# Two residual blocks in one kernel: the entry of the last FFN with its additions on two engines and its first round of gate and up in two merged steps

## The chip, the cores and the metric

The kernel runs on one core of one Trainium2 chip. The metric is device microseconds of one execution, and the time of a kernel is the median of several executions. The time before the change is 1148.94 us, the median of three executions (1146.13, 1148.94 and 1149.74). The profile is of a separate execution.

## The reference, cut to what matters

The reference chains two transformer blocks over 256 tokens of width 1024, all in float32. The first has two layers (an HGRN2 mixer, a band attention, and an FFN in each) and a final norm. The second has four attention mixers side by side, an output projection, and a convolutional FFN, which is the last thing computed. The change lies between that projection and the first products of this FFN:

```python
def _conv_ffn(x, w_gate, w_up, conv_w, conv_b, w_down):
    a = x @ w_gate                                   # 1024 x 4096
    a = lax.conv_general_dilated(a, conv_w[:, None, :], (1,), [(2, 0)], ...) + conv_b
    return (jax.nn.gelu(a, approximate=True) * (x @ w_up)) @ w_down

x = x + _rms_norm(mix @ w_out[l], attn_post_norm[l])
h = _rms_norm(x, ffn_pre_norm[l])
x = x + _rms_norm(_conv_ffn(h, ffn_w_gate[l], ffn_w_up[l], ffn_conv_w[l], ffn_conv_b[l], ffn_w_down[l]),
                  ffn_post_norm[l])
```

## The kernel before

**Split operands.** Every float32 product is made of three: an operand is split into a high part in a reduced format (hi) and the rest (lo), and PE computes hi·hi, hi·lo and lo·hi into the same PSUM bank (`mm3`, L257 to L260). Activations stand transposed, 128 features by 256 tokens in each of eight pieces k.

**Weight units and their pipeline.** Weights come as units of 128x1024 numbers. SP starts the DMA of a unit into one of seven raw buffers; ScalarE casts it to `w_hi` (L193) and VectorE subtracts to get `w_lo` (L195), each into one of four buffers. The program is a list of steps, each with the units it needs. `pump` runs before each step and emits the casts of units to come: it goes on while the number of units cast is at most `AHEAD` = 2 above the number of units used by the steps already emitted. So three units lie ready at any step, and the casts stand in the queues of ScalarE and VectorE at the place where the step before ended. Nothing reorders them after that: each engine works its queue in the order of the program.

**The FFN.** `ffn` makes 16 rounds. In round r, `lin_A` gives gate two steps and up two steps of one unit each (24 matmuls, k = 0 to 3 and then 4 to 7). When gate is complete, `conv_gate` runs: in round 0 it first calls `f2_scale`, which sums the squares of the residual on PE (`stat_mm`, L463) and takes 1/rms on ScalarE (L468, L469); then VectorE scales the gate (L1771), ScalarE and VectorE make the convolution (L1776 to L1779). `conv_gelu` (L1784 on ScalarE, L1786 on GpSimd) is emitted ahead of the first step of up. When up is complete, `mul_hidden` multiplies (L1073) and splits the hidden values (L1063, L1064). The down products of round r-1 follow those of round r.

**The entry.** `f2_start` (L1734) ends the projection: 1/rms of the mixer's output, then for each k the normed piece `nt` on VectorE (L1747, its source in PSUM), its addition to the residual on GpSimd (L1749), the high part on ScalarE (L1750) and, two pieces later, the low part on VectorE (L1752). Four squares of the residual on ScalarE follow (L1756), for `f2_scale`.

Of the kernel before, what the change touches and what calls it, by code (L numbers as in the profile page):

```python
# [10 lines left out]
F32 = mybir.dt.float32  # L11
F32R = mybir.dt.float32r
I32 = mybir.dt.int32
AF = mybir.ActivationFunctionType
OP = mybir.AluOpType
AX = mybir.AxisListType

P = 128
D = 1024
KT = 8  # L20
# [111 lines left out]
def kernel(ctx: ExitStack, tc: tile.TileContext, x, c, mod_w, mod_b, norm_mix, norm_ffn,  # L132
# [9 lines left out]
    PE, DV, SC, GP, SY = nc.tensor, nc.vector, nc.scalar, nc.gpsimd, nc.sync  # L142
# [12 lines left out]
    def bank(tag="b", bufs=3):  # L155
        return ps.tile([P, 512], F32, name="pb_" + tag, tag=tag, bufs=bufs)

    def acc_bank():
        return bank("acc", 4)
# [10 lines left out]
    def small(w, name, bufs=2, dt=F32):  # L170
        return wk.tile([P, w], dt, name=name, tag=name, bufs=bufs)
# [73 lines left out]
    def unit_A(w, r0, c0, k=4, width=256):  # L245
        ap = w[r0:r0 + k * P, c0:c0 + width].rearrange("(k p) m -> p k m", p=P)
        return Unit(k, width, [(0, width, ap)])
# [14 lines left out]
    def lin_A(w, c0, act, evac, alloc=bank):  # L262
        box = {}

        def half(i, u):
            if i == 0:
                box["p"] = alloc()
            p = box["p"]
            xhi, xlo = act()
            for k in range(4):  # L270
                for m in range(2):
                    mm3(p[:, 256 * m:256 * m + 256], u.hi[:, k, P * m:P * m + P], u.lo[:, k, P * m:P * m + P],
                        xhi[:, 4 * i + k], xlo[:, 4 * i + k], i == 0 and k == 0 and m == 0, i == 1 and k == 3)
            if i == 1:
                evac(p)

        return [Step(lambda u: half(0, u), [unit_A(w, 0, c0)], 2.6),
                Step(lambda u: half(1, u), [unit_A(w, 512, c0)], 2.6)]

    def lin_B(w, c0, act, evac):  # L280
        box = {}
# [88 lines left out]
    for n, ap in vb_list:  # L370
        r = rows(ap)
# [4 lines left out]
    def vcol(n):  # L376
        o, r, _ = VB[n]
        return vb_t[:, o:o + r]
# [7 lines left out]
    def hT():  # L386
        return hbox["h"]
# [201 lines left out]
    def act(tag):  # L589
        return lambda: ubox[tag]  # L590
# [437 lines left out]
    def ffn(w_gate, c_gate, w_up, c_up, w_out, rounds, u, gated, hidden, down, down_last, mid=None):  # L1028
        HB = {}
        gu = []  # L1030
        for r in range(rounds):
            def ev_gate(p, r=r):
                HB[r] = gated(r, p)

            def ev_up(p, r=r):
                HB[r] = hidden(r, HB[r], p)
            gate, up = lin_A(w_gate, c_gate + 256 * r, u, ev_gate), lin_A(w_up, c_up + 256 * r, u, ev_up)
            if mid:
                up[0].before = lambda r=r: mid(HB[r])
            gu.append(gate + up)  # L1040
        box = {}

        def dn(r, i, un):
            if r == 0 and i == 0:
                box["a"] = [acc_bank() for _ in range(4)]
            hi, lo = HB[r]
            down(box["a"], un, hi[:, i], lo[:, i], r == 0 and i == 0)

        def dn_last(ua, ub):
            down_last(box["a"], (ua, ub), HB[rounds - 1])  # L1050

        st = list(gu[0])
        for r in range(1, rounds):
            st += gu[r]
            for i in range(2):
                st.append(Step(lambda un, r=r, i=i: dn(r - 1, i, un), [unit_row(w_out, 256 * (r - 1) + P * i)], 2.6))
        st.append(Step(dn_last, [unit_row(w_out, 256 * (rounds - 1) + P * i) for i in range(2)], 5.2))
        return st

    def split_hidden(r, hid):  # L1060
        h = slot(5 + 2 * (r % 2), F32R)
# [215 lines left out]
    for i, g in ((2, g12[NF:]), (3, gemv_mod(1, 3, gemv_w)), (4, gemv_mod(1, 4, gemv_w))):  # L1277
        m = sum(len(s.units) for s in g)
# [12 lines left out]
    B_ = {}  # L1291
# [442 lines left out]
    def f2_start():  # L1734

        st = bank()
        stat_mm(st, stF[3], 0)
        PE.matmul(st[:, 0:256], lhsT=mean_d, rhs=stF[0][:, 0:256], start=False, stop=True)
        r = rstd_of(st[:, 0:256])
        hi = slot(1, F32R).rearrange("p (k t) -> p k t", k=KT)  # L1740
        lo = slot(2, F32R).rearrange("p (k t) -> p k t", k=KT)
        ubox["f2"] = (hi, lo)
        pre = vcol("ffn_pre")
        for k in range(KT + 2):
            if k < KT:
                t = small(256, "nt", 3)
                DV.scalar_tensor_tensor(t, B_["y", k // 2][:, 256 * (k % 2):256 * (k % 2) + 256],  # L1747
                                        vcol("attn_post")[:, k:k + 1], r, op0=OP.mult, op1=OP.mult)
                GP.tensor_add(hT()[:, k], hT()[:, k], t)  # L1749
                SC.activation(hi[:, k], hT()[:, k], AF.Identity, scale=pre[:, k:k + 1])  # L1750
            if k > 1:
                DV.scalar_tensor_tensor(lo[:, k - 2], hT()[:, k - 2], pre[:, k - 2:k - 1],  # L1752
                                        hi[:, k - 2].bitcast(F32), op0=OP.mult, op1=OP.subtract)
        for j in range(4):
            stF[j] = ph(768, "att", 4)[:, 0:512]
            SC.activation(stF[j], hT()[:, 2 * j:2 * j + 2].rearrange("p k t -> p (k t)"), AF.Square)  # L1756
# [135 lines left out]
```

## Time and profile before

| | |
|---|---|
| median of three executions | 1148.94 us (1146.13 to 1149.74) |
| the profiled execution | 1142.66 us, of which the span from the first to the last instruction is 1140.9 us |
| granted TensorE clock, mean over the span | 0.994 |
| busy in the span: PE, VectorE, ScalarE, GpSimd | 1098.1, 763.4, 573.4, 138.1 us |
| waits of PE for the entry's operand (L1750) | 2.9 us |

The profile names engines PE (TensorE; PEld is its weight load), DVE (VectorE), ACT (ScalarE), POOL (GpSimd) and SP (SyncE, which starts the weight DMAs). In its timeline a row has the start in us from the span's first instruction, the duration, engine, line, operation, the tiles out<-in, the shape, the count of merged instructions, and in brackets how long the engine sat idle before and what ended that. Matmuls overlap each other, so their pitch is shorter than their duration. A float32 matmul of `stat_mm` is two instructions in the profile.

### The profile page before, as it was taken

The numbers are of one execution on the slowest core, as the hardware profiler recorded it, in microseconds if no ns is written. First come the engines' busy times: TensorE is split into PE (matmuls) and PEld (weight loads), VectorE is DVE, ScalarE is ACT, GpSimd is POOL, SyncE is SP. The second block draws the span as 40 slices with busy tenths as digits, with TensorE's granted clock in tenths as the row PEclk, the third lists the DMA queues.
The fourth block names the chain that finished last, engine by engine and source line by source line (L and its number), as shares of the span: only waits on it lengthen the run. The fifth ranks groups of instructions, "written<-read, shape, count | busy, mean of one in ns | idle before, by whom it ended". The sixth has DMA issues, their size and how long they took to land.

```text
span 1140.9 us, 23598 instructions
## 1 busy us (share of the span) xinstructions
PE 1098.1 (96%) x9689; PEld 1014.4 (89%) x9689; DVE 763.4 (67%) x1237; ACT 573.4 (50%) x913; POOL 138.1 (12%) x201
## 2 busy tenths in 40 slices
PE   6988999999999999999999999999999999999997
PEld 4885789899999979888999999988888999999997
DVE  3586765787787688885564454667766766666666
ACT  3455464644444566555444444646555544554454
POOL 4044400000000001250000000013312100000000
PEclk9998999999999999999999999999999999999999
DMA  9976777798988777865766556773343656555651
GB/s 276 318 262 205 224 223 239 257 298 305 302 280 298 232 237 234 292 239 170 237 197 209 185 188 169 153 214 112 116 145 94 217 183 191 186 183 185 192 178 56
DMA packets 176125, 241.92 MB, mean 212 GB/s; under 512 B 18713, under 2 KB 142161, under 8 KB 176017
## 3 DMA queue, kind: packets, MB, share of 16 engines
q1 hardware_dynamic: 174928, 239.54, 66.4%
q8 instruction: 76, 1.25, 0.4%
q0 software_dynamic: 912, 0.81, 0.3%
q14 instruction: 33, 0.26, 0.1%
q10 hardware_dynamic: 176, 0.07, 0.0%
HBM read 239.33 MB, written 1.05 MB: 211 GB/s over the span
## 4 chain that ended last, share of the span: by engine, by line
PE 82%; DVE 6%; DMA 4%; ACT 4%; issue 2%; POOL 1%; SPq 0%; DVEq 0%; ACTq 0%; POOLq 0%
PE pb_b L258 14%; PE pb_b L260 14%; PE pb_b L259 14%; PE pb_acc L258 11%; PE pb_acc L260 10%; PE pb_acc L259 10%; DVE w_lo L195 2%; DMA w_raw<-in_a_w_in_dram 2%; ACT w_hi L193 2%; PE pb_b L463 1%; PE pb_b L1216 1%; DMA w_raw<-in_mod_w_dram 1%; DMA w_raw<-in_kv_w_dram 1%; PE pb_gv L524 1%; DVE nt L573 1%
## 5 line engine op out<-in xcount | busy, mean ns | idle before, releaser
L195 DVE TENSOR_TENSOR w_lo<-w_raw,w_hi 128x1024 fp32r<-128x1024 f32 (+1 forms) x335 | 409.3, 1246 | 172.7 <-ACT w_hi L193 172.0
L258 PE MATMUL pb_b<-s,w_hi 128*128 128x256 f32 x1488 | 419.4, 282 | 5.1 <-ACT s L1750 2.9
L260 PE MATMUL pb_b<-s,w_lo 128*128 128x256 f32 x1488 | 416.2, 280 | 1.6 <-DVE w_lo L195 1.5
L259 PE MATMUL pb_b<-s,w_hi 128*128 128x256 f32 x1488 | 417.3, 280 | 0.3
L193 ACT CAST w_hi<-w_raw 128x1024 fp32r<-128x1024 f32 (+1 forms) x336 | 342.1, 1043 | 79.3 <-DMA w_raw<-in_a_w_in_dram 19.2
L258 PEld LDWEIGHTS pb_b<-s,w_hi 128*128 128x128 f32 x1488 | 280.3, 188 | 12.7 <-issue 4.0
L260 PEld LDWEIGHTS pb_b<-s,w_lo 128*128 128x128 f32 x1488 | 280.3, 188 | 2.6 <-DVE w_lo L195 2.6
L259 PEld LDWEIGHTS pb_b<-s,w_hi 128*128 128x128 f32 x1488 | 280.3, 188 | 1.9 <-DVE s L585 0.7
L260 PE MATMUL pb_acc<-s,w_lo 128*128 128x256 f32 x656 | 183.4, 280 | 4.0 <-DVE w_lo L195 4.0
L258 PE MATMUL pb_acc<-s,w_hi 128*128 128x256 f32 x656 | 186.7, 285 | 0.6 <-ACT w_hi L193 0.6
L259 PE MATMUL pb_acc<-s,w_hi 128*128 128x256 f32 x656 | 183.1, 279 | 0.0
L258 PEld LDWEIGHTS pb_acc<-s,w_hi 128*128 128x128 f32 x656 | 123.3, 188 | 5.8 <-issue 3.5
L260 PEld LDWEIGHTS pb_acc<-s,w_lo 128*128 128x128 f32 x656 | 123.3, 188 | 4.8 <-DVE w_lo L195 4.8
L259 PEld LDWEIGHTS pb_acc<-s,w_hi 128*128 128x128 f32 x656 | 123.4, 188 | 0.2
L1209 POOL TENSOR_SCALAR att<-att,sm 128x128 f32<-128x128 f32 (+1 forms) x72 | 46.7, 668 | 619.4 <-DVE sm L1202 337.7
L1063 ACT CAST s<-sig 128x512 fp32r<-128x512 f32 x38 | 23.6, 621 | 115.9 <-DVE sig L1073 115.9
L258 PE MATMUL pb_acc<-w_hi,s 128*128 128x512 f32 x192 | 78.3, 408 | 1.7 <-ACT s L579 1.0
L259 PE MATMUL pb_acc<-w_lo,s 128*128 128x512 f32 x192 | 76.6, 399 | 0.8 <-DVE w_lo L195 0.8
L260 PE MATMUL pb_acc<-w_hi,s 128*128 128x512 f32 x192 | 76.5, 399 | 0.0
L1776 ACT ACTIVATE sig<-att,vb_t,vc_t 128x256 f32<-128x256 f32 x32 | 17.5, 595 | 75.4 <-DVE att L1771 75.4
L1069 ACT ACTIVATE sig<-pb_b 128x512 f32<-128x512 f32 x22 | 13.2, 598 | 77.8 <-PE pb_b L260 77.7
L1786 POOL TENSOR_TENSOR sig<-sig,rstd 128x512 f32<-128x512 f32 x16 | 22.7, 1420 | 237.2 <-ACT sig L1784 237.2
(373 smaller groups left out, 1255.7 us busy)
## 6 DMA issues: line engine op xcount, KB each, us to landing
w_raw<-in_mod_w_dram SPq DMA_DIRECT2D x96, 512.0 KB, 4.9
w_raw<-in_ffn_w_in_dram SPq DMA_DIRECT2D x88, 512.0 KB, 5.2
w_raw<-in_ffn_w_out_dram SPq DMA_DIRECT2D x44, 512.0 KB, 4.8
w_raw<-in_a_w_in_dram SPq DMA_DIRECT2D x32, 512.0 KB, 5.5
w_raw<-in_ffn_w_gate_dram SPq DMA_DIRECT2D x32, 512.0 KB, 3.8
w_raw<-in_ffn_w_up_dram SPq DMA_DIRECT2D x32, 512.0 KB, 5.3
w_raw<-in_ffn_w_down_dram SPq DMA_DIRECT2D x32, 512.0 KB, 3.6
w_raw<-in_kv_mod_w_dram SPq DMA_DIRECT2D x16, 512.0 KB, 5.8
```

Source lines behind the costliest of these rows:

```text
L193: SC.copy(hi, raw)
L195: DV.tensor_sub(lo, raw, hi.bitcast(F32))
L258: PE.matmul(o, lhsT=whi, rhs=xhi, start=start, stop=False, skip_group_check=True)
L259: PE.matmul(o, lhsT=whi, rhs=xlo, start=False, stop=False, skip_group_check=True)
L260: PE.matmul(o, lhsT=wlo, rhs=xhi, start=False, stop=stop, skip_group_check=True)
L463: PE.matmul(st[:, 0:256], lhsT=mean_d, rhs=sq[:, 256 * m:256 * m + 256], start=j == 0 and m == 0, stop=j == n - 1 and m == 1)
L524: PE.matmul(g[32 * j:32 * j + 32, 0:256], lhsT=by, rhs=r, start=start, stop=stop, tile_position=(0, 32 * j))
L1063: SC.copy(hi, hid)
L1069: SC.activation(sg, g, AF.Silu)
L1209: GP.tensor_scalar(t[:, i, cs], t[:, i, cs], r[:, 2 * b + i:2 * b + i + 1], 1.0, op0=OP.mult, op1=OP.mult)
L1776: SC.activation(zm, am, AF.Identity, bias=vcol("conv_b")[:, f:f + 1], scale=vc_t[:, 64 + f:65 + f])
L1786: GP.tensor_mul(zp, zp, rs_pair())
```

## The change

In `f2_start` the additions to the residual alternate: even pieces on VectorE, odd ones on GpSimd. The low parts are no longer made two pieces behind: those of pieces 0 to 3 come together after the fifth addition, those of 4 to 7 at the end. In the FFN with a `mid` function (the last one), the four steps of round 0 become two. Step i takes the units of gate and of up for four k at once, first all products with the high part of the operand (for gate and up, with both parts of the weights), then those with its low part. What followed each complete product (`conv_gate` with `f2_scale`, `conv_gelu`, `mul_hidden`) now comes in that order at the end of the second step.

```diff
@@ lin_A
-        return [Step(lambda u: half(0, u), [unit_A(w, 0, c0)], 2.6),
-                Step(lambda u: half(1, u), [unit_A(w, 512, c0)], 2.6)]
+        st = [Step(lambda u: half(0, u), [unit_A(w, 0, c0)], 2.6),
+              Step(lambda u: half(1, u), [unit_A(w, 512, c0)], 2.6)]
+        for s_ in st:
+            s_.evac = evac
+        return st
@@ ffn
         st = list(gu[0])
+        if mid:
+            st = [first_round(w_gate, c_gate, w_up, c_up, u, i, gu[0]) for i in range(2)]
...
+    def first_round(w_gate, c_gate, w_up, c_up, act, i, gu):
+
+        def f(ug, uu):
+            xhi, xlo = act()
+            for part in range(2):
+                for k in range(4):
+                    for u, n in ((ug, 0), (uu, 1)):
+                        if i == 0 and part == 0 and k == 0:
+                            first_bank[n] = bank()
+                        for m in range(2):
+                            o = first_bank[n][:, 256 * m:256 * m + 256]
+                            whi, wlo = (w[:, k, P * m:P * m + P] for w in (u.hi, u.lo))
+                            x_ = xhi[:, 4 * i + k]
+                            if part == 0:
+                                PE.matmul(o, lhsT=whi, rhs=x_, start=i == 0 and k == 0 and m == 0, stop=False,
+                                          skip_group_check=True)
+                                PE.matmul(o, lhsT=wlo, rhs=x_, start=False, stop=False, skip_group_check=True)
+                            else:
+                                PE.matmul(o, lhsT=whi, rhs=xlo[:, 4 * i + k], start=False, stop=i == 1 and k == 3,
+                                          skip_group_check=True)
+            if i == 1:
+                gu[0].evac(first_bank[0])
+                gu[2].before()
+                gu[2].evac(first_bank[1])
+        return Step(f, gu[i].units + gu[2 + i].units, 5.2)
@@ f2_start
-        for k in range(KT + 2):
-            if k < KT:
-                t = small(256, "nt", 3)
...
-                GP.tensor_add(hT()[:, k], hT()[:, k], t)
-                SC.activation(hi[:, k], hT()[:, k], AF.Identity, scale=pre[:, k:k + 1])
-            if k > 1:
...
+        for k in range(KT):
+            t = small(256, "nt", 3)
...
+            (GP if k % 2 else DV).tensor_add(hT()[:, k], hT()[:, k], t)
+            SC.activation(hi[:, k], hT()[:, k], AF.Identity, scale=pre[:, k:k + 1])
+            if k == 4:
+                for n in range(4):
+                    low(n)
+        for n in range(4, KT):
+            low(n)
```

In the order of VectorE at the entry (`nt` is the normed piece, `s0` the residual, `s1` and `s2` the high and the low part of the operand), there stood before:

```order
L1747 SCALAR_TENSOR_TENSOR nt_10461<-pb_acc_10118,vb_t_78,rstd_10456 128x256
L1747 SCALAR_TENSOR_TENSOR nt_10465<-pb_acc_10118,vb_t_78,rstd_10456 128x256
L1747 SCALAR_TENSOR_TENSOR nt_10469<-pb_acc_10119,vb_t_78,rstd_10456 128x256
L1752 SCALAR_TENSOR_TENSOR s2_10460<-s0_171,vb_t_78,s1_10459 128x256
L1747 SCALAR_TENSOR_TENSOR nt_10474<-pb_acc_10119,vb_t_78,rstd_10456 128x256
```

and there stand now:

```order
L1784 SCALAR_TENSOR_TENSOR nt_10461<-pb_acc_10118,vb_t_78,rstd_10456 128x256
L1786 TENSOR_TENSOR s0_171<-s0_171,nt_10461 128x256
L1784 SCALAR_TENSOR_TENSOR nt_10465<-pb_acc_10118,vb_t_78,rstd_10456 128x256
L1784 SCALAR_TENSOR_TENSOR nt_10469<-pb_acc_10119,vb_t_78,rstd_10456 128x256
L1786 TENSOR_TENSOR s0_171<-s0_171,nt_10469 128x256
L1784 SCALAR_TENSOR_TENSOR nt_10473<-pb_acc_10119,vb_t_78,rstd_10456 128x256
L1784 SCALAR_TENSOR_TENSOR nt_10477<-pb_acc_10120,vb_t_78,rstd_10456 128x256
L1786 TENSOR_TENSOR s0_171<-s0_171,nt_10477 128x256
L1779 SCALAR_TENSOR_TENSOR s2_10460<-s0_171,vb_t_78,s1_10459 128x256 x4
L1784 SCALAR_TENSOR_TENSOR nt_10485<-pb_acc_10120,vb_t_78,rstd_10456 128x256
```

Four additions came to VectorE, and four low parts now stand together ahead of the sixth normed piece.

In the order of ScalarE behind the entry's squares, `w_hi` of raw buffer 10202 is the second unit of up of round 0, that of 10251 and 10291 the first and second unit of gate of round 1, that of 10340 the first of up of round 1; `sig` is the gate on its way through convolution and gelu, `s5` the split hidden. Before:

```order
L1756 ACTIVATE att_10507<-s0_171 128x512
L193 CAST w_hi_10534<-w_raw_10202 128x1024
L468 ACTIVATE rstd_10573<-pb_b_10564,epsc_87 128x256
L469 ACTIVATE rstd_10573<-rstd_10573 128x256
L1776 ACTIVATE sig_10578<-att_10576,vb_t_78,vc_t_79 128x256 x2
L193 CAST w_hi_10585<-w_raw_10251 128x1024
L1784 ACT_TABLE_LOAD
L1784 ACTIVATE sig_10578<-sig_10578 128x512
L193 CAST w_hi_10618<-w_raw_10291 128x1024
L1063 CAST s5_10649<-sig_10578 128x512
L193 CAST w_hi_10652<-w_raw_10340 128x1024
```

and now:

```order
L1795 ACTIVATE att_10507<-s0_171 128x512
L193 CAST w_hi_10559<-w_raw_10202 128x1024
L193 CAST w_hi_10565<-w_raw_10251 128x1024
L471 ACTIVATE rstd_10628<-pb_b_10619,epsc_87 128x256
L472 ACTIVATE rstd_10628<-rstd_10628 128x256
L1815 ACTIVATE sig_10633<-att_10631,vb_t_78,vc_t_79 128x256 x2
L1823 ACT_TABLE_LOAD
L1823 ACTIVATE sig_10633<-sig_10633 128x512
L1096 CAST s5_10643<-sig_10633 128x512
L193 CAST w_hi_10646<-w_raw_10291 128x1024
L193 CAST w_hi_10652<-w_raw_10340 128x1024
```

The cast of the first unit of gate of round 1 moved ahead of the 1/rms, and that of the second unit (10291) moved behind the gelu and behind the cast of the hidden values.

In the order of PE at the start of the second merged step, whose first unit of weights is gate (10446) and whose second is up (10559), with their banks 10509 and 10514, there stand now:

```order
L1081 MATMUL pb_b_10509<-s1_10459,w_hi_10446 128x256
L1083 MATMUL pb_b_10509<-s1_10459,w_lo_10447 128x256
L1081 MATMUL pb_b_10509<-s1_10459,w_hi_10446 128x256
L1083 MATMUL pb_b_10509<-s1_10459,w_lo_10447 128x256
L1081 MATMUL pb_b_10514<-s1_10459,w_hi_10559 128x256
L1083 MATMUL pb_b_10514<-s1_10459,w_lo_10560 128x256
```

Before, this unit of up was first used 48 matmuls of round 0 and the sum of squares later than the operand's fifth piece; now it is used four matmuls after it.

More of the change, by code (lines that the diff above doesn't have):

```diff
@@ L1058, in ffn @@
         return st
+    first_bank = {}
+    def first_round(w_gate, c_gate, w_up, c_up, act, i, gu):
[22 more added lines that the diff above has]
+        return Step(f, gu[i].units + gu[2 + i].units, 5.2)
     def split_hidden(r, hid):
@@ L1743, in f2_start, with low @@
         pre = vcol("ffn_pre")
-        for k in range(KT + 2):
-            if k < KT:
-                t = small(256, "nt", 3)
[L1747 to L1750, printed above, removed]
-            if k > 1:
-                DV.scalar_tensor_tensor(lo[:, k - 2], hT()[:, k - 2], pre[:, k - 2:k - 1],
-                                        hi[:, k - 2].bitcast(F32), op0=OP.mult, op1=OP.subtract)
+        def low(k):
+            DV.scalar_tensor_tensor(lo[:, k], hT()[:, k], pre[:, k:k + 1], hi[:, k].bitcast(F32), op0=OP.mult,
+                                    op1=OP.subtract)
+        for k in range(KT):
+            t = small(256, "nt", 3)
+            DV.scalar_tensor_tensor(t, B_["y", k // 2][:, 256 * (k % 2):256 * (k % 2) + 256],
+                                    vcol("attn_post")[:, k:k + 1], r, op0=OP.mult, op1=OP.mult)
+            (GP if k % 2 else DV).tensor_add(hT()[:, k], hT()[:, k], t)
[5 more added lines that the diff above has]
+            low(n)
         for j in range(4):
```

## The prediction

> **What bounds the kernel now.** I read the page's busy times and its chain first, then a table of windows around the last FFN's entry, then the timeline there row by row.
>
> ```profile
> span 1140.9 us, 23598 instructions
> PE 1098.1 (96%) x9689; PEld 1014.4 (89%) x9689; DVE 763.4 (67%) x1237; ACT 573.4 (50%) x913; POOL 138.1 (12%) x201
> PE 82%; DVE 6%; DMA 4%; ACT 4%; issue 2%; POOL 1%; SPq 0%; DVEq 0%; ACTq 0%; POOLq 0%
> ```
>
> PE is busy 96% of the span and carries 82% of the chain. Time that PE loses is lost for good unless a later stage has slack. Here are windows from the entry on; in each row stand the stretch, then busy time and count of PE, PEld, DVE, ACT and POOL, then the granted TensorE clock.
>
> ```profile
> 855.00:857.88 2.88, 0.00 (x1) 0.00 (x1) 1.86 (x5) 1.40 (x3) 1.32 (x2) 0.96 0.40 117
> 857.88:860.91 3.03, 3.03 (x12) 2.80 (x13) 3.03 (x8) 1.72 (x4) 3.03 (x5) 0.50 0.16 65
> 860.91:865.20 4.29, 4.29 (x37) 4.29 (x37) 2.89 (x7) 3.18 (x7) 2.42 (x3) 0.98 0.00 0
> 865.20:868.47 3.27, 3.27 (x19) 2.88 (x17) 1.23 (x1) 1.69 (x3) 0.00 (x0) 1.00 0.00 0
> 868.47:874.00 5.53, 5.53 (x48) 5.50 (x47) 3.44 (x6) 3.76 (x6) 0.00 (x0) 1.00 0.30 95
> 900.00:1130.00 230.00, 230.00 (x1635) 214.47 (x1634) 155.08 (x178) 113.78 (x141) 19.92 (x14) 1.00 0.54 173
> ```
>
> The entry costs one idle stretch of 2.88 us and then a stretch at clock 0.50 in which only 12 matmuls issue in 3.03 us. At full clock a matmul takes 4.29 / 37 = 0.116 us. From there PE is never idle: gate until 865.20, the sum of squares until 868.47, then up. In the last row PE is busy 230.00 of 230.00 us, so what is lost at the entry is not made up later. All that the change can win lies in these 2.88 us and the slow stretch, some 4.5 us at most.
>
> **The entry.** Its first rows, and then the durations of its lines (ns, shortest, median and longest of eight; the last two rows are groups with count, busy us and mean ns):
>
> ```profile
> 855.99 1.27 DVE L1747 SCALAR_TENSOR_TENSOR nt<-pb_acc,vb_t,rstd 128x256 f32<-128x256 f32 x3 [0.42 <-ACT rstd L469]
> 856.56 6.77 POOL L1749 TENSOR_TENSOR s<-s,nt 128x256 f32<-128x256 f32 x8 [17.60 <-DVE nt L1747]
> 857.32 0.51 ACT L1750 ACTIVATE s<-s,vb_t 128x256 fp32r<-128x256 f32 x1 [1.36 <-POOL s L1749]
> 857.88 0.58 PE L258 MATMUL pb_b<-s,w_hi 128*128 128x256 f32 x1 [2.88 <-ACT s L1750]
> ```
> ```profile
> L1749 POOL TENSOR_TENSOR s<-s,nt x8: 725/916/1009, 856.6 to 862.4; 128x256 f32<-128x256 f32 x8
> L1752 DVE SCALAR_TENSOR_TENSOR s<-s,vb_t,s x8: 483/559/585, 857.9 to 863.9; 128x256 fp32r<-128x256 f32 x8
> L1747 DVE SCALAR_TENSOR_TENSOR nt<-pb_acc,vb_t,rstd 128x256 f32<-128x256 f32 x8 | 3.6, 476 | 0.4 <-ACT rstd L469 0.4
> L1730 DVE TENSOR_TENSOR sq<-sq 128x256 f32<-128x256 f32 x1 | 0.4, 426 | 0.0
> ```
>
> An addition of this shape on DVE has one row, 0.43 us (L1730). The first operand now comes after 0.48 (nt) + 0.43 (add) + 0.51 (high part) plus three gaps of 0.05: PE starts at 857.55 instead of 857.88. Its 48 products of the first step no longer wait for low parts. Up to about 860.9 they run at half clock (0.23 each), some 15 of them, and 33 follow at 0.116: the step ends near 864.75, where the first 48 ended at 865.20. **Gain 0.45 us.** An addition with POOL beside it has no row; L1752, which also has two inputs in SBUF, goes from 0.48 to 0.56 us and at most 0.59, so an addition takes 0.43 to 0.53, and the four together up to 0.4 us more.
>
> Work moved on DVE delays the end of the entry. Ahead of the last POOL addition DVE does 8 nt at a pitch of 0.40 (three in 1.27), 4 additions and 4 low parts at about 0.48: 3.2 + 1.9 + 1.9 = 7.0, to 863.0. That addition takes 0.73 to 1.01 (median 0.92), so the last high part starts near 863.95. Before, it started at 863.36, as the first row here shows:
>
> ```profile
> 863.36 0.51 ACT L1750 ACTIVATE s<-s,vb_t 128x256 fp32r<-128x256 f32 x1 [0.37 <-POOL s L1749]
> 863.78 2.17 ACT L1756 ACTIVATE att<-s 128x512 f32<-128x512 f32 x4
> 865.86 1.03 ACT L193 CAST w_hi<-w_raw 128x1024 fp32r<-128x1024 f32 x1
> 866.92 1.23 DVE L195 TENSOR_TENSOR w_lo<-w_raw,w_hi 128x1024 fp32r<-128x1024 f32 x1 [2.53 <-ACT w_hi L193]
> ```
>
> [...]
>
> **First new wait: the second unit of up.** Its cast is the third row above and its low part the fourth. They keep their place in the queues, behind the four squares, but PE now wants them four matmuls into the second step, at 864.75 + 4 × 0.116 = 865.2. The squares move 0.6 us later with the last high part, so w_hi starts at 866.45 and w_lo ends at 866.92 + 0.6 + 1.23 = 868.75. PE issues one product with w_hi in between and then waits to 868.8. **Loss 3.5 us**; from both sides, 2.9 (no delay of the squares) and 4.5 (0.4 for slower additions, 0.6 for low parts and a last piece at their slowest). Behind the waiting product stand the rest of the second step, the sum of squares, and all rounds after.
>
> **Order of the sum of squares.** PE does 43 more products, 5.0 us, to 873.8, and then the sum (3.27 us, its window above) to 877.05. In the chain that follows I read the rows of before:
>
> ```profile
> 868.85 0.48 ACT L468 ACTIVATE rstd<-pb_b,epsc 128x256 f32<-128x256 f32 x1 [1.97 <-PE pb_b L463]
> 869.82 0.69 DVE L1771 TENSOR_TENSOR att<-pb_b,rstd 128x512 f32<-128x512 f32 x1 [1.67 <-ACT rstd L469]
> 870.54 1.09 ACT L1776 ACTIVATE sig<-att,vb_t,vc_t 128x256 f32<-128x256 f32 x2 [0.76 <-DVE att L1771]
> 872.61 0.48 DVE L1779 SCALAR_TENSOR_TENSOR sig<-att,vc_t,sig 128x254 f32<-128x254 f32 x1
> 873.17 1.28 ACT L1784 ACT_TABLE_LOAD   x1 [0.60 <-DVE sig L1779]
> 874.47 0.63 ACT L1784 ACTIVATE sig<-sig 128x512 f32<-128x512 f32 x1
> 875.18 1.31 POOL L1786 TENSOR_TENSOR sig<-sig,rstd 128x512 f32<-128x512 f32 x1 [11.85 <-ACT sig L1784]
> 877.49 0.67 DVE L1073 TENSOR_TENSOR sig<-sig,pb_b 128x512 f32<-128x512 f32 x1
> 878.20 0.62 ACT L1063 CAST s<-sig 128x512 fp32r<-128x512 f32 x1 [2.15 <-DVE sig L1073]
> ```
>
> The logarithm (first row) started 0.38 after the sum's window ended, so it now starts at 877.45. The next gate goes into the bank from which it reads, so PE waits for its end, 877.95. Before, up ran on PE during all this chain; now only one unit of round 1 is ready, 24 products, 2.8 us, to 880.75.
>
> **Second new wait: the second unit of gate of round 1.** Its cast now stands behind the whole chain. From the start of the logarithm to the end of the GpSimd product it is 875.18 + 1.31 - 868.85 = 7.64 us. The multiplication (0.67) and the cast of the hidden values (0.62) follow at once, 0.04 apart, since no w_lo stands ahead of them any more; then w_hi (1.03) and w_lo (1.23), 0.05 apart each: 7.64 + 0.71 + 0.66 + 1.08 + 1.28 = 11.4, less 0.1 by which two ACT instructions overlap. PE has its first low product of that unit at 877.45 + 11.3 = 888.75. Before:
>
> ```profile
> 877.62 0.39 PE L260 MATMUL pb_b<-s,w_lo 128*128 128x256 f32 x1
> 881.08 0.39 PE L260 MATMUL pb_b<-s,w_lo 128*128 128x256 f32 x1 [0.36 <-DVE w_lo L195]
> ```
>
> The same product issued at 877.62, so **PE is 11.1 us later** here (3.5 - 0.45 of the first wait, the rest of the second, some 8 us of idle PE less the 0.5 of the logarithm's wait). The small wait of the second row goes (0.5 with its restart), since the later units are then cast ahead: 10.6. DMAs take no part, as SP's last row ahead of the entry shows:
>
> ```profile
> 849.49 6.45 SPq L186 DMA_DIRECT2D w_raw<-in_ffn_w_down_dram  x2
> ```
>
> By then SP has started the units of down that follow round 1, so round 1's own were started before; those of round 2 start when w_lo of the units above frees their buffers, and have over 10 us.
>
> **The clock.** Two waits of PE earlier in the program show when it drops:
>
> ```profile
> 81.07:83.52 2.45, 0.00 (x0) 0.03 (x1) 2.42 (x5) 0.66 (x1) 1.29 (x1) 1.00 0.70 200
> 83.52:87.00 3.48, 3.48 (x65) 3.31 (x69) 2.83 (x6) 0.70 (x2) 1.01 (x1) 1.00 0.51 182
> 100.91:104.53 3.62, 0.00 (x0) 0.00 (x1) 2.34 (x8) 3.35 (x7) 0.00 (x0) 0.83 0.50 179
> 104.53:110.00 5.47, 5.47 (x80) 3.99 (x81) 3.41 (x6) 1.70 (x6) 4.24 (x4) 0.50 0.55 169
> ```
>
> After 2.45 us idle it stayed at 1.00, after 3.62 it was 0.50 for 5.5 us, and after the entry's 2.88 for 3 us. Half clock for 3 us loses 1.5, for 5.5 up to 2.7. The second wait surely drops it: 1.7, between 0.3 and 2.7. The first wait is cut in two by one product, about 2.1 and 1.1 us, so I charge two thirds of 1.5: 1.0, between 0 and 1.7. [...]
>
> **Sum.** 10.6 + 1.7 + 1.0 = 13.3 us. Against the profiled execution (1140.9 span, 1142.66 in all) that is 1156. The median of before, 1148.94, lies 6.3 above that execution; I carry this distance over: 1148.94 + 13.3 = 1162.2, 1.2% slower. With the bounds of the parts, 9 to 17 us on 1146 to 1150: 1155 to 1167.
>
> **Rivals.**
> (1) PE stays fed and the shorter entry shows: 0.45 us, and up to 1.5 if the shorter idle stretch keeps the clock up: 1147 to 1148.5. It needs w_lo of up at 865.2 instead of 868.75 and that of round 1's gate at 880.75 instead of 888.75. For it speaks that PE's 2.88 us are real; against it that both casts are queued behind work whose times are measured. Chance 2% for faster by over 0.3% (3.4 us, about what a measurement of this kernel can tell from no change), 2% for within it.
> (2) Only the first wait is real: the chain is hidden because the units are cast earlier than I read the order. 3.5 - 0.45 + 1.0 + 0.5: +4.6, 1153.5. Against it: the cast of 10291 stands behind that of the hidden values. 3%.
> (3) Only the second wait is real: the squares come much earlier, for instance since the additions on DVE free POOL. +8.5, 1157.5. 4%.
> (4) [...] 6%.
> (5) The entry does not get shorter, since the second piece waits behind an addition on DVE: 0.45 more, 1162.6; it lies in the forecast.
>
> The forecast itself has 83%. With (3), and half of (2) and (4), the range is 1153.5 to 1167. Faster 0.02, same 0.02, slower 0.96.
>
> **What would show it.** In the profile after: PE starts near 857.55; waits of some 2 and 1 us for w_hi and w_lo four products into the second merged step; a 0.5 us wait for the logarithm; then one of about 7 us for ACT w_hi L193 and 1 for DVE w_lo, with a clock of 0.50 behind it. I am wrong if PE's waits between 857 and 890 add up to less than 8 us, or if a later stage takes the loss back.

## The result and the profile after

| | before | after |
|---|---|---|
| median of six executions each | 1148.38 us (1145.58 to 1149.74) | 1162.51 us (1157.67 to 1165.54) |
| ratio to before, 95% interval | | 1.0124 [1.0106, 1.0143] |
| the profiled execution, its span | 1142.66 us, 1140.9 us | 1162.22 us, 1160.4 us |
| granted TensorE clock, mean over the span | 0.994 | 0.986 |

The change makes the kernel 1.24% slower, some 14 us; 1162.2 us had been predicted. The page of after has these lines for the span, the busy times and the chain:

```profile
span 1160.4 us, 23595 instructions
PE 1106.5 (95%) x9689; PEld 1021.9 (88%) x9689; DVE 765.1 (66%) x1241; ACT 573.4 (49%) x913; POOL 135.4 (12%) x197
PE 81%; DVE 6%; DMA 5%; ACT 5%; issue 2%; POOL 1%; SPq 0%; DVEq 0%; ACTq 0%; POOLq 0%
```

PE has as many instructions as before, DVE four more and POOL four fewer. To see where the time went I cut both spans at the same two events: the first normed piece of the entry, and the first product of down of round 0. In these windows stand the stretch, then busy time and count of PE, PEld, DVE, ACT and POOL, then the granted clock; first before, then after.

```profile
0.00:855.99 855.99, 821.41 (x7737) 756.68 (x7737) 572.91 (x1006) 431.19 (x724) 108.10 (x176) 1.00 0.72 227
855.99:886.55 30.56, 28.22 (x208) 27.17 (x209) 20.83 (x34) 18.56 (x29) 8.47 (x10) 0.94 0.34 103
886.55:1140.90 254.35, 248.44 (x1746) 230.51 (x1744) 169.66 (x197) 123.68 (x161) 21.55 (x16) 0.99 0.54 174
```
```profile
0.00:860.26 860.26, 824.51 (x7737) 759.53 (x7737) 572.59 (x1007) 431.41 (x724) 109.05 (x176) 0.99 0.72 226
860.26:906.13 45.87, 33.61 (x209) 31.91 (x209) 23.26 (x39) 18.67 (x29) 5.76 (x6) 0.81 0.23 69
906.13:1160.40 254.27, 248.43 (x1746) 230.51 (x1744) 169.29 (x197) 123.31 (x160) 20.59 (x16) 1.00 0.55 174
```

The two profiled executions differ by 19.5 us. Of these, 4.3 arose ahead of the entry, over the same 7737 matmuls, at a clock that was slightly lower (0.99 against 1.00): that is a difference between two executions, not of the change (two of the runs below that leave everything ahead of the entry as before reached it at 859.79 and 863.47). **The stretch from the entry to down is 15.3 us longer** (45.87 against 30.56), and behind it nothing is taken back or lost (254.27 against 254.35). I call these middle rows "the stretch"; the experiments are read by its length, since it leaves out what varies ahead of it.

PE's timeline of after has these rows in that stretch, with the start of the sum of squares and of down; in brackets stands how long PE was idle before, and what ended that:

```profile
872.25 0.42 PE L1081 MATMUL pb_b<-s,w_hi 128*128 128x256 f32 x1 [2.54 <-ACT w_hi L193]
873.51 0.58 PE L1083 MATMUL pb_b<-s,w_lo 128*128 128x256 f32 x1 [0.84 <-DVE w_lo L195]
881.27 3.61 PE L466 MATMUL pb_b<-att,early 128*128 128x256 f32 x16
885.45 0.39 PE L258 MATMUL pb_b<-s,w_hi 128*128 128x256 f32 x1 [0.57 <-ACT rstd L471]
894.87 0.58 PE L258 MATMUL pb_b<-s,w_hi 128*128 128x256 f32 x1 [6.32 <-ACT w_hi L193]
896.13 0.58 PE L260 MATMUL pb_b<-s,w_lo 128*128 128x256 f32 x1 [0.46 <-DVE w_lo L195]
906.13 0.40 PE L258 MATMUL pb_acc<-w_hi,s 128*128 128x512 f32 x1
```

Five of the seven rows end an idle time of PE that before did not have: a first wait for the second unit of up (2.54 and 0.84), one for the logarithm (0.57), and a second wait for the second unit of gate of round 1 (6.32 and 0.46). All five end with a cast (`w_hi`, `w_lo`) or the logarithm, none with a DMA. Windows of the same stretch show what the clock did behind the waits, the first being the idle time of the entry:

```profile
859.26:861.79 2.53, 0.00 (x1) 0.00 (x0) 2.08 (x5) 1.40 (x3) 0.11 (x1) 1.00 0.39 60
861.79:865.65 3.86, 3.85 (x19) 3.86 (x20) 3.79 (x9) 1.82 (x4) 1.35 (x2) 0.56 0.24 99
...
873.00:880.70 7.70, 7.19 (x39) 7.19 (x40) 1.60 (x2) 0.15 (x1) 0.00 (x0) 0.59 0.44 136
...
895.00:900.00 5.00, 4.54 (x21) 4.24 (x22) 3.35 (x3) 1.71 (x2) 0.00 (x0) 0.52 0.50 152
900.00:906.00 6.00, 6.00 (x53) 6.00 (x52) 4.03 (x7) 3.60 (x5) 1.25 (x1) 1.00 0.40 136
```

The clock is at 0.56, 0.59 and 0.52 behind each of the three waits. Behind the first new wait (third row) only 39 matmuls issue in 7.70 us; in the last row, at full clock, 53 issue in 6.00.

### The profile page after: what moved, and what is told of

Same layout as the page of the kernel before. It is cut to its first block, busy times and chain, and to the rows that moved or that the text cites. A ratio compares the mean times of both kernels' runs of the same rounds, so it can differ in the third digit from the quotient of the medians.

```text
span 1160.4 us, 23595 instructions
## 1 busy us (share of the span) xinstructions
PE 1106.5 (95%) x9689; PEld 1021.9 (88%) x9689; DVE 765.1 (66%) x1241; ACT 573.4 (49%) x913; POOL 135.4 (12%) x197
## 4 chain that ended last, share of the span: by engine, by line
PE 81%; DVE 6%; DMA 5%; ACT 5%; issue 2%; POOL 1%; SPq 0%; DVEq 0%; ACTq 0%; POOLq 0%
PE pb_b L258 14%; PE pb_b L260 14%; PE pb_b L259 14%; PE pb_acc L258 10%; PE pb_acc L260 10%; PE pb_acc L259 10%; DMA w_raw<-in_a_w_in_dram 2%; DVE w_lo L195 2%; ACT w_hi L193 2%; PE pb_b L466 1%; DMA w_raw<-in_kv_w_dram 1%; DMA w_raw<-in_mod_w_dram 1%; PE pb_gv L527 1%; PE pb_b L1249 1%; ACT att L1225 1%
## 5 line engine op out<-in xcount | busy, mean ns | idle before, releaser
L258 PE MATMUL pb_b<-s,w_hi 128*128 128x256 f32 x1456 | 410.7, 282 | 9.7 <-ACT w_hi L193 6.3
L260 PE MATMUL pb_b<-s,w_lo 128*128 128x256 f32 x1456 | 407.4, 280 | 1.6 <-DVE w_lo L195 1.6
L259 PE MATMUL pb_b<-s,w_hi 128*128 128x256 f32 x1456 | 408.5, 281 | 0.3
L258 PEld LDWEIGHTS pb_b<-s,w_hi 128*128 128x128 f32 x1456 | 274.6, 189 | 17.5 <-ACT w_hi L193 6.9
L260 PEld LDWEIGHTS pb_b<-s,w_lo 128*128 128x128 f32 x1456 | 274.5, 189 | 2.3 <-DVE w_lo L195 2.3
L259 PEld LDWEIGHTS pb_b<-s,w_hi 128*128 128x128 f32 x1456 | 274.6, 189 | 1.6 <-DVE s L588 0.7
```

The source lines that it names most:

```text
L258: PE.matmul(o, lhsT=whi, rhs=xhi, start=start, stop=False, skip_group_check=True)
L259: PE.matmul(o, lhsT=whi, rhs=xlo, start=False, stop=False, skip_group_check=True)
L260: PE.matmul(o, lhsT=wlo, rhs=xhi, start=False, stop=stop, skip_group_check=True)
```

## The experiments

The theory was the prediction's: two casts now stand behind work that PE needs them ahead of, and the clock drops behind PE's idle time on top, as it had to 0.50 behind the 2.88 us at the entry of before. The rivals were that the additions on VectorE make the loss, and that the clock makes most of it. All ratios are to before, run on the same chip.

**The entry alone.** Before, with `f2_start` of after.

```diff
+            (GP if k % 2 else DV).tensor_add(hT()[:, k], hT()[:, k], t)
...
+            if k == 4:
+                for n in range(4):
+                    low(n)
+        for n in range(4, KT):
+            low(n)
```

> The kernel before with the new entry alone: residual additions by turns on VectorE and GpSimd, low parts later, but gate and up in their four old steps. My theory (the loss sits in two units of weights that PE asks for before they are cast): about 1 us more than before (0.5 to 2.5), since gate's second product now waits for the first low part, some 2.5 us after the first product, and gate ends about 0.8 us later; no wait of PE for w_hi. Rival A (the entry is what loses: work moved to VectorE delays the operand): 8 us or more. The stretch from the first normed piece to the first product of down, 30.6 us before and 45.9 us after the change, should be 31 to 33 us by my theory and over 38 us by rival A.

Measured: 1.0025 [1.0007, 1.0043]; the stretch is 33.89 us, 3.3 longer than before and a little above the 31 to 33 expected. Its list of PE's waits (us in total, times, longest) has a new row:

```profile
PE pb_b L259 <- DVE s L1746: 2.4, 1, 2.4
```

PE starts 0.35 us earlier, as in after, but the old order of products wants low parts within its first products, and they are now made four pieces late: 2.4 us of waiting. Behind it PE's products issue 0.21 us apart up to 873.5, 5.7 us after the wait ends at 867.83, and then 0.12 apart; in before the clock was at 0.50 for 3.4 us (857.66 to 861.07). So the new entry needs products in another order, and alone it costs a fifth of what the whole change costs.

**The merge alone.** After, with `f2_start` of before.

```diff
-            (GP if k % 2 else DV).tensor_add(hT()[:, k], hT()[:, k], t)
+                GP.tensor_add(hT()[:, k], hT()[:, k], t)
...
+            if k > 1:
+                DV.scalar_tensor_tensor(lo[:, k - 2], hT()[:, k - 2], pre[:, k - 2:k - 1],
+                                        hi[:, k - 2].bitcast(F32), op0=OP.mult, op1=OP.subtract)
```

> The changed kernel with the old entry: additions on GpSimd alone, low parts two pieces behind, but gate and up of round 0 merged. My theory: some 13 us more than before (11 to 15), 1 us less than the full change, because the last high part and with it the squares and the cast of up's second unit come about 1 us earlier, and so the first wait is 1 us shorter. The stretch from the first normed piece to the first product of down: 43.5 to 45.5 us. Rival A: within 2 us of before.

Measured: 1.0128 [1.0093, 1.0163], the whole loss; the stretch is 44.60 us.

```profile
PE pb_b L258 <- ACT w_hi L193: 6.4, 1, 6.4
...
PE pb_b L1081 <- ACT w_hi L193: 1.1, 1, 1.1
```

Both new waits are there with the additions back on GpSimd. The additions on VectorE are not the cause.

**The squares behind the casts.** After, with the four squares in a step of no units between the two merged steps, so that the casts ahead of that step come first on ScalarE.

```diff
+    def f2_squares():
         for j in range(4):
...
+            st.insert(1, Step(f2_squares, [], 0.0))
```

> The changed kernel with the four squares of the residual put behind the casts of the two units that follow them on ScalarE. My theory: up's second unit is cast 2.2 us earlier, so PE's first wait (2.5 for w_hi and 0.8 for w_lo) shrinks to about 1.2 us in all, and the clock probably keeps its full rate behind it; the second wait stays at 6 to 7 us. Against the full change 2.2 us less, and up to 5 us less where the clock stays up: 9 to 12 us more than before. Rival B (PE's first wait is for VectorE, which is busy with low parts, or for the operand): the wait keeps its length and the time that of the full change, 14 us more than before.

Measured: 1.0107 [1.0090, 1.0124]; the stretch is 41.61 us, 4.3 shorter than after's.

```profile
PE pb_b L258 <- ACT w_hi L193: 6.3, 1, 6.3
...
PE pb_b L1082 <- ACT w_hi L193: 0.5, 1, 0.5
```

The first wait falls from 2.5 to 0.5 for the high part of the weights, with 0.88 for the low part, and the products behind it issue 0.12 us apart, as at full clock; the second stays at 6.3. So the squares' place in ScalarE's queue makes the first wait's larger half. The rest is the cast and its low part, which now follow the last high part at once. The time is some 12 us above before, where 9 to 12 were expected: behind the second wait, which ends at 892.15, the products issue 0.21 us apart up to 898.1, for 5.9 us, where in after the clock was at 0.50 for 4.9 us behind that wait (894.87 to 899.78).

**Casts between the evacuations.** After, with one more unit cast behind `conv_gate` and one more behind `conv_gelu` at the end of the second merged step, instead of all behind `mul_hidden`.

```diff
                 gu[0].evac(first_bank[0])
+                state["used_w"] += 1
+                pump()
                 gu[2].before()
+                state["used_w"] += 1
+                pump()
                 gu[2].evac(first_bank[1])
+                state["used_w"] -= 2
```

> The changed kernel with the casts of round 1's second gate unit and first up unit put back where they stood before the change: the first behind the two activations of conv_gate, the second behind the gelu, ahead of the cast of the hidden values. My theory: the second unit of gate is there 5.5 us after the start of the logarithm and not 11.2, so that PE's wait of 6.3 us for w_hi falls to about 1 and with w_lo to 2.5 us; smaller waits of 1 to 2 us come with the next units, since the chain is now held up by two casts; net 4 us less than the full change, 9 to 11 us more than before. Rival C (what holds round 1 is the sum of squares and its chain behind up, not the casts): the time stays that of the full change, 14 us more than before.

Measured: 1.0084 [1.0065, 1.0104]; the stretch is 39.38 us, 6.5 shorter than after's, and the part behind it 1.6 longer (255.95).

```profile
PE pb_b L1081 <- ACT w_hi L193: 2.6, 1, 2.6
...
PE pb_b L260 <- DVE w_lo L195: 1.8, 3, 1.2
PE pb_acc L259 <- DVE w_lo L195: 1.2, 1, 1.2
```

The second wait has gone but for 1.8 us in three pieces, with no instruction taken away: it was the place of the cast behind the chain from logarithm to hidden values. The first wait stays. A new one of 1.2 appears at down; it is explained below.

**Both.** The two edits together.

> The changed kernel with both places of the casts mended: the squares behind the casts of up's second unit, and round 1's casts put between the pieces of the chain. My theory: the two savings add, since they lie at different waits. The stretch from the first normed piece to the first product of down was 45.9 us with the change, the sum of squares' logarithm started 20.0 us after the first normed piece with the squares behind, and from that logarithm to down it took 14.9 us with the casts between: 34.9 us, 4.3 us more than the 30.6 of before, and up to 1.6 more behind it, where a later unit came late with the casts between. So 4 to 7 us more than before. A rival that some third cause holds 4 us or more would see over 39 us in the stretch.

Measured: 1.0047 [1.0026, 1.0068]; the stretch is 36.41 us. The two edits save 4.3 and 6.5 alone, which would give 35.1; the other 1.3 fits 16 products behind the first wait, from 874.34 to 877.72, which issue 0.21 us apart in this execution and 0.12 apart in that of the squares' edit alone. With both casts moved, 0.77 of the 1.24% are gone.

**The clock alone.** After, with products of constant tiles that nothing reads, put ahead of each wait: 5 at the entry, 11 ahead of the second unit of up, 14 ahead of the second unit of gate of round 1.

```diff
+    def fill(n):
+        o = bank("gv", 1)
+        for i in range(n):
+            PE.matmul(o[:, 0:256], lhsT=mean_d, rhs=early, start=True, stop=True)
...
+                        if i == 1 and part == 0 and k == 0 and n == 1:
+                            fill(11)
```

> The changed kernel with products of two constant tiles, whose result nothing reads, put on PE in the entry's idle stretch (5), ahead of up's second unit (11) and ahead of round 1's second gate unit (14). They make no wait shorter; what changes is that PE is busy. My theory: the clock stays at its full rate, and the change then costs the waits alone: 2.8 us less after the first wait and 1.8 less after the second, so a stretch of 41 us (40 to 42.5) against 45.9, and 9 to 11 us more than before instead of 14. Rival D (the low clock does not come from PE's idleness, or costs nothing): the stretch stays at 45 us or grows by the added products.

Measured: 1.0095 [1.0077, 1.0113]; the stretch is 41.51 us. Two of its windows, behind the first and the second wait:

```profile
872.40:881.00 8.60, 8.47 (x59) 7.98 (x59) 1.21 (x2) 0.00 (x0) 0.00 (x0) 1.00 0.41 124
...
891.80:900.80 9.00, 8.28 (x71) 8.28 (x71) 7.04 (x10) 4.91 (x7) 1.32 (x1) 1.00 0.55 177
```

The clock is at 1.00 from 860.82 to 900.80, and 4.4 of the 15.3 us go (45.87 less 41.51). **So the clock is a bit under a third of the stretch's loss, and the waits by themselves are 11 us.**

**Clock at the entry of before.** Before, with 6 such products in its entry's idle time.

> The kernel before with six products of constant tiles in the entry's idle stretch of 2.9 us, nothing else. The clock should stay up there. My theory: this alone wins almost nothing, since the old gate cannot run ahead of its operand: the last low part lands 8.4 us after the first normed piece whatever the clock, and gate ended 9.2 us after it, so at most 0.3 us less; stretch to down 30.2 to 30.6 us against 30.56, ratio 0.999 to 1.001. Rival E (the half clock of the entry costs its full 1.5 us in the kernel before): stretch 29 us, ratio 0.9985 to 0.999, clearest in the stretch.

Measured: 0.9993 [0.9976, 1.0010], no difference. The stretch is 30.51 us, as before's 30.56, though the clock doesn't drop at its entry:

```profile
858.64:861.68 3.04, 2.75 (x13) 2.10 (x12) 2.02 (x5) 1.40 (x3) 1.32 (x2) 1.00 0.39 96
861.68:869.00 7.32, 7.18 (x49) 6.32 (x50) 5.93 (x13) 4.89 (x10) 5.45 (x7) 1.00 0.08 33
```

PE at full clock reaches the end of gate at 868.95, 9.16 us behind the first normed piece (before 9.21), because the entry's operand comes piece by piece until then. The half clock that the profile of before shows at its entry is paid by nobody.

**Only the first half merged.** After, with the first merged step kept (k = 0 to 3 of gate and up), and then gate's second unit with its evacuation and up's second unit as steps of their own, so that the sum of squares and the chain behind it run beside up again; one more unit is cast behind the gelu.

```diff
-            st = [first_round(w_gate, c_gate, w_up, c_up, u, i, gu[0]) for i in range(2)]
+            st = [first_round(w_gate, c_gate, w_up, c_up, u, 0, gu[0])] + [second_half(n, u, gu[0]) for n in range(2)]
```

> The idea of the change with the weights asked for in the order in which they are cast: first the merged step of gate and up for the first four pieces, then gate's second unit alone with the sum of squares and conv_gate behind it, then up's second unit; one more unit (round 1's first of up) is cast behind the gelu. My theory: both new waits vanish, since 24 products and the sum of squares lie ahead of up's second unit and 48 products behind the logarithm; PE starts 0.35 us earlier. The stretch from the first normed piece to the first product of down: 29.5 to 31.5 us, so the time of before within 1 us. Rival A (the entry's additions and late low parts cost by themselves): over 33 us.

Measured: 1.0011 [0.9999, 1.0023]; the stretch is 29.06 us, 1.5 shorter than before's, and what follows is 1.5 longer (255.89).

```profile
PE pb_acc L259 <- DVE w_lo L195: 1.2, 1, 1.2
```

Both new waits are gone from the list. This row of it shows where the gain of the shorter entry ends: at the low part of down's first unit. VectorE's rows ahead of it, of this kernel and then of before:

```profile
884.90 0.68 DVE L1837 TENSOR_TENSOR att<-pb_b,rstd 128x512 f32<-128x512 f32 x1
...
888.09 1.22 DVE L195 TENSOR_TENSOR w_lo<-w_raw,w_hi 128x1024 fp32r<-128x1024 f32 x1
```
```profile
882.08 0.68 DVE L1771 TENSOR_TENSOR att<-pb_b,rstd 128x512 f32<-128x512 f32 x1
...
885.27 1.22 DVE L195 TENSOR_TENSOR w_lo<-w_raw,w_hi 128x1024 fp32r<-128x1024 f32 x1
```

From the scaling of the gate to the end of that low part VectorE takes 4.41 us in both (884.90 to 889.31, 882.08 to 886.49). Before, down began at 886.55, just behind; here PE has down's first product at 887.73 and waits 1.16. Most of what PE wins ahead of this point (1.5) is lost again at it.

**The same with the clock kept up**, with 5 products that nothing reads in the entry's idle time.

> The kernel with three steps and five products of constant tiles in the entry's idle stretch of 2.5 us, so that the clock does not drop there. My theory: 1.5 us less than with three steps alone in those executions in which the clock dropped at the entry: a stretch of 28 to 30 us, 1 to 2 us less than before (ratio 0.998 to 0.9995). Rival D: no difference to three steps alone.

Measured: 0.9992 [0.9979, 1.0005], the stretch 29.06 us as without them: in the profile of the kernel without them the clock had stayed at 1.00 by itself (860.21 to 865.00, behind 2.53 us idle). Of all versions this is the best, but it can't be told from before. Its median is 2.7 us below that of the kernel without the products (1146.58 against 1149.28), as would be expected if the clock drops there in other executions; no profile shows one that does.

**All additions on VectorE.** After, without GpSimd at the entry.

```diff
-            (GP if k % 2 else DV).tensor_add(hT()[:, k], hT()[:, k], t)
+            DV.tensor_add(hT()[:, k], hT()[:, k], t)
```

> The changed kernel with all eight additions to the residual on VectorE, GpSimd none; everything else as it is. In the changed kernel three additions on VectorE took 0.67 us, each with a GpSimd addition beside it, the first, with none beside it, took 0.42, and one low part beside a GpSimd addition took 0.96 where seven others took 0.47. Theory (the two engines hold each other up): all eight additions take 0.42 and all eight low parts 0.47. VectorE then needs 8 x 0.40 for the normed pieces, 8 x 0.35 for additions and 4 x 0.39 for low parts ahead of the last high part, 7.6 us: that part starts 7.6 to 7.7 us behind the first normed piece, where it started 8.42 behind it, and the first wait ends 0.75 earlier, 12.5 behind it instead of 13.25. Rival (an addition that follows a normed piece of another buffer takes 0.67 in any case): the last high part starts near 9 us, and the first wait ends 0.6 later than in the changed kernel. The second wait, and the time of the whole to within 1 us but for the clock, stay by both: near 1.0120 of before by the theory, 1.0130 by the rival, which the time alone can hardly tell apart; the durations do.

Measured: 1.0142 [1.0096, 1.0188]; the stretch is 45.56 us, with the waits of after. The durations of the additions and of the low parts in this kernel (ns, shortest, median, longest), and then those of the additions in after:

```profile
L1786 DVE TENSOR_TENSOR s<-s,nt x8: 424/424/426, 860.6 to 868.2; 128x256 f32<-128x256 f32 x8
L1779 DVE SCALAR_TENSOR_TENSOR s<-s,vb_t,s x8: 477/478/482, 864.3 to 869.7; 128x256 fp32r<-128x256 f32 x8
```
```profile
L1786 DVE TENSOR_TENSOR s<-s,nt x4: 424/670/673, 860.8 to 866.6; 128x256 f32<-128x256 f32 x4
```

The durations decide for the theory: 0.42 and 0.48 us for all eight. What they were to bring didn't come, and the first wait didn't get shorter (2.69 and 0.68 us): the last high part starts 8.54 us behind the first normed piece, not 7.6, since each addition now waits for its own piece (0.51 from the start of a piece to the start of its addition, where two pieces follow each other at 0.40).

## Why the prediction was right, step by step

Measured from the first normed piece, with the prediction's own points moved to the same zero (855.99):

| point | predicted | measured |
|---|---|---|
| PE starts | 1.56 | 1.53 |
| end of the first merged step | 8.76 | 8.82 |
| last high part starts | 7.96 | 8.42 |
| end of the first wait | 12.81 | 13.25 |
| from there to the logarithm | 8.65, and 1.0 for the clock | 11.42 |
| from the logarithm to round 1's low product | 11.3 | 11.2 |
| from there to down (before 8.93) | 10.1 | 10.0 |
| the stretch against before | +13.3 | +15.3 |

**The entry** became shorter as said, and the gain was worth nothing on its own. That part of the prediction's ceiling was too generous: it counted the slow clock of before as time that the change could win, and the run of before with a full clock there shows that it isn't. The shorter entry can win at most the 1.5 us of the version with one merged step, until down's low part takes it back.

**The first wait** came where it was predicted, for the cast and the low part of up's second unit, and the run with the squares behind the casts shows that the squares hold the cast up. It ended 0.44 us later than forecast, inside its bounds. The step that was off is VectorE's work ahead of GpSimd's last addition, which was charged 7.0 us and took 7.47 (860.26 to 867.73). These rows of after show it, first of VectorE and ScalarE, then of GpSimd:

```profile
860.77 0.42 DVE L1786 TENSOR_TENSOR s<-s,nt 128x256 f32<-128x256 f32 x1
862.02 0.67 DVE L1786 TENSOR_TENSOR s<-s,nt 128x256 f32<-128x256 f32 x1
...
864.11 1.66 DVE L1779 SCALAR_TENSOR_TENSOR s<-s,vb_t,s 128x256 fp32r<-128x256 f32 x4
865.69 0.86 DVE L1784 SCALAR_TENSOR_TENSOR nt<-pb_acc,vb_t,rstd 128x256 f32<-128x256 f32 x2
...
868.68 0.51 ACT L1787 ACTIVATE s<-s,vb_t 128x256 fp32r<-128x256 f32 x1 [0.75 <-POOL s L1786]
...
871.17 1.97 ACT L193 CAST w_hi<-w_raw 128x1024 fp32r<-128x1024 f32 x2
```
```profile
861.68 0.73 POOL L1786 TENSOR_TENSOR s<-s,nt 128x256 f32<-128x256 f32 x1 [18.43 <-DVE nt L1784]
```

The first addition runs alone and takes 0.42. The second starts while GpSimd's first is under way (861.68 to 862.41) and ends 0.28 behind it; the other two end 0.28 and 0.29 behind theirs. An addition had been charged 0.43 to 0.53; counted from start to start, the four took 2.13 instead of 1.9. The larger error is in the normed pieces, charged 0.40 each: one with its addition right behind it has 0.50 to itself, and the eight took 3.76 instead of 3.2. The first four low parts gave some of it back (1.58 from 864.11 to 865.69, instead of 1.9). Together that is the 0.46 by which the last high part is late. From there the rows run as predicted: four squares from 869.10 on, then the casts.

**The clock behind the first wait** is the term that was mis-sized. It was charged 1.0 us, since the wait is cut in two by one product. The 43 products from 873.51 to the sum of squares at 881.27 took 7.76 us instead of 5.0: 2.8 us, because the half clock lasted 6.83 us, not about 3. That is outside the bounds of 0 to 1.7 that the prediction gave the term. This one step explains 1.8 of the 2.0 us by which the stretch exceeds the forecast. Windows that end where the clock changed (872.47 and 879.30), and halfway between, show how it came about:

```profile
869.06:872.47 3.41, 0.87 (x7) 0.64 (x5) 0.90 (x3) 3.41 (x7) 0.00 (x0) 1.00 0.00 0
872.47:875.88 3.41, 2.57 (x12) 2.37 (x12) 2.13 (x2) 0.68 (x1) 0.00 (x0) 0.50 0.33 92
875.88:879.30 3.42, 3.42 (x18) 3.42 (x18) 0.00 (x0) 0.00 (x0) 0.00 (x0) 0.50 0.67 215
```

In after's stretch the clock changes at 862.23, 865.65, 872.47, 879.30, 892.95 and 899.78 us: 3.41 us apart, or twice or four times that. The 2.54 us of waiting for the high part lie ahead of 872.47, where the clock is halved. The 0.84 us of waiting for the low part lie behind it, and the clock stays low until 879.30. So the one product between the two pieces, for which the prediction lowered its charge, saved nothing here: 2.8 us are lost, where an uncut wait had been counted at 1.5. The run with casts between the evacuations, whose first wait has two pieces as well (2.56 and 0.68), shows the same: the products stay 0.21 us apart up to 875.7, 6.7 us after the wait for the high part ends at 868.95. What sets the length of the low clock no run shows. The cost isn't the same in every execution: the run with the squares moved shows that a shorter wait (0.49 and 0.88 us) can leave the clock up, and the executions of after spread over 8 us, where the lower mean clock goes with the longer time (0.990 with 1157.67 us, 0.982 with 1165.54). Their median, 14.1 us above that of before, stands between the forecast and the profiled stretch.

**The order of the sum of squares and the second wait** came out to a tenth of a microsecond: 0.57 for the logarithm, 6.32 and 0.46 for the unit of gate, 11.2 from the logarithm to the low product. In ScalarE's rows the chain stands ahead of the cast as the order had shown:

```profile
884.93 0.47 ACT L471 ACTIVATE rstd<-pb_b,epsc 128x256 f32<-128x256 f32 x1 [11.78 <-PE pb_b L466]
...
889.24 1.28 ACT L1823 ACT_TABLE_LOAD   x1 [1.54 <-DVE sig L1818]
...
893.26 0.62 ACT L1096 CAST s<-sig 128x512 fp32r<-128x512 f32 x1 [2.09 <-DVE sig L1106]
893.78 2.93 ACT L193 CAST w_hi<-w_raw 128x1024 fp32r<-128x1024 f32 x3
```

ScalarE itself is idle for most of it; the casts wait only because they stand behind in the queue. The run with casts between the evacuations shows that the queue's order makes this wait, all but the 1.8 us for low parts that are left there. PE's delay without the clock was put at 10.6; with the clock at 1.00 in both kernels the stretches differ by 41.51 - 30.51 = 11.0.

**The rivals.** That PE stays fed (1), or that one of the waits is hidden (2 and 3), falls by the list of waits. No run shows the +18 us of the fourth, half of whose 6% the range counts: VectorE and GpSimd do hold each other up (an addition of VectorE took 0.67 us beside one of GpSimd and 0.42 alone), and the clock was low for 6.83 us behind the first wait, but the stretch lost 15.3 us. The fifth falls, since the first merged step ends at 8.82, where the first 48 products of before ended at 9.21. No run shows a further cost of the merge or the entry. What is left with both casts moved (36.41 against 30.56) holds the shorter first wait, 1.8 us for low parts, products 0.21 us apart behind the entry (up to 867.4) and behind the first wait (up to 877.7), and the 0.6 for the logarithm, which no longer lies beside up. How these 5.9 us divide was not tried one by one.

**The distance of the median** from the profiled execution was carried over (6.3 us). The profile of before was a short execution, that of after an ordinary one (1162.22 against a median of 1162.51), and the 4.3 us that differ ahead of the entry are most of that distance. That the time came out within 0.3 us of the forecast is partly luck: the loss was 0.8 us larger than forecast (14.1 against 13.3), and the median of before, now of six executions, 0.6 lower than the one that the forecast started from.

## What to carry to other kernels

When steps are merged under a prefetch that looks a fixed number of units ahead, count what the merged step's end puts into the queues: every cast for the next step now stands behind all its evacuations, and an idle engine doesn't help a cast that stands behind a waiting one. Reduce an idle stretch of the bounding engine only after asking whether the work behind it is bound by its operands: here the half clock at the old entry cost nothing (a stretch of 30.56 us with it, 30.51 without), and a shorter entry ran into VectorE's queue 30 us later. Read a change of one place by the stretch between two fixed events, since the spans of two executions differed by 4.3 us ahead of it.

## What the runs showed of the hardware

**VectorE and GpSimd hold each other up.** Of the four additions that VectorE makes in after, the first, with none of GpSimd beside it, took 0.42 us; the other three each start beside one of GpSimd, took 0.67, and end 0.28 to 0.29 us after that ends. It shows in before too, where the six low parts that start from 858.66 to 863.02, each beside a GpSimd addition, took 0.56 to 0.58 us, and the last one, with none beside it, 0.48; of one of the six:

```profile
858.90 0.91 POOL L1749 TENSOR_TENSOR s<-s,nt 128x256 f32<-128x256 f32 x1
859.54 0.56 DVE L1752 SCALAR_TENSOR_TENSOR s<-s,vb_t,s 128x256 fp32r<-128x256 f32 x1
```

The two end at 859.81 and 860.10. In after one low part that starts beside the last GpSimd addition took 0.96 and the other seven 0.47. With no GpSimd addition, all eight additions took 0.42 and all eight low parts 0.48. The two durations don't add up whole, though: in before the additions of GpSimd from 858.90 on start 0.87 to 0.89 us apart, each with a low part beside it, while an addition took 0.73 and a low part 0.48 where they stood alone, 1.21 together. How the two engines come to hold each other up no run shows.

**The same idle time may or may not cost the clock.** After's entry idles for 2.53 us and runs on at 0.56. The version with one merged step idles for 2.53 at its entry too (857.68 to 860.21), and runs on at full clock:

```profile
857.68:860.21 2.53, 0.00 (x1) 0.01 (x1) 2.08 (x5) 1.40 (x3) 0.12 (x1) 1.00 0.40 62
860.21:865.00 4.79, 4.78 (x38) 4.58 (x39) 4.69 (x12) 1.82 (x4) 1.70 (x3) 1.00 0.19 79
```

The idle 2.45 us at 81.07 in before left the clock at 1.00 too, and the 2.88 us at its entry did not (0.50 from 857.66 to 861.07). So the length of an idle time alone doesn't tell in these traces whether the clock drops; what does, no run shows.

In after's stretch the clock was at 0.50 for 3.41 us behind the entry (862.23 to 865.65) and for 6.83 us at either wait (872.47 to 879.30 and 892.95 to 899.78).
